# A two-layer retention / mLSTM trunk: 38 groups of mixer projections rewritten as seven half-size products, with one pool of weight tiles

## The chip, the cores and the metric

The kernel runs on one core of one Trainium2 chip. The metric is the device time of one execution in microseconds (us), as the median of several runs. PE is TensorE (PEld its weight loads), DVE is VectorE, ACT is ScalarE, POOL is GpSimd, SP is SyncE, which issues most DMAs.

## The reference

A residual stream `x` of 512 positions by 1024 channels passes two layers. Each has a token mixer (layer 0: retention, layer 1: mLSTM) and a convolutional feed-forward net (FFN). Each of the four is normalised and modulated by the condition `c`:

```
mod = silu(c) @ ada_w[i] + ada_b[i]                 # 6 x 1024 modulations of a layer
h   = rmsnorm(x, norm_tok_g[i]) * (1 + sc_t) + sh_t
x   = x + gt_t * mixer(h)                           # retention or mLSTM, 4 heads
h   = rmsnorm(x, norm_ffn_g[i]) * (1 + sc_f) + sh_f
x   = x + gt_f * (silu(a) * b) @ w_down             # a, b = causal_dwconv(h @ w_up)
```

A mixer projects `h` to queries and keys (256 columns a head each), values and gates (512 columns a head each), forms causal scores (512 by 512), weights the values with them, normalises by head, gates, and multiplies with `w_out`. The change touches only how the projections `h @ w_in` of the mixers are computed, and where the modulations stand.

## The kernel before

**Number format.** Every float32 operand is split into a high part, rounded to the type that PE multiplies in one pass (`F32R`), and a low part, the rest. A product is three matmuls: high by high, high by low, low by high (`mm3`, line 585). For weights, ACT rounds the high part (`high_part`, 467) and DVE subtracts it from the loaded tile (`low_part`, 472). `low_part_added` (477) makes the low part without DVE: ACT writes minus the high part, and a DMA issued by POOL adds the loaded tile to it.

**Two ways to project.** `proj_item` (673) makes 128 output channels for all 512 positions: 8 slices of the contraction, three matmuls each, 24 matmuls 512 wide. Before, all queries, keys and gates of the mixers go this way. `v_items` (819) makes the 512 value columns of a head with 96 matmuls 512 wide. In the FFN, `folded` (682) takes two weight tiles at a time and halves positions and contraction, and computes the four quarter products by seven products of half size and sums (the Strassen-Winograd scheme): per product 4 slices and three matmuls 256 wide, so 84 for a pair of tiles. `Fold` (518) prepares its weights: sums of halves on DVE (`ws`, `wt`), three rounded tiles on ACT, low parts mostly by `low_part_added`. The sums of `h` that it needs (`t24`, `t3`) come from `Start.sums` (982) and `turn` (1005). After some products ACT copies a partial result out of PSUM (`fs`) and DVE adds it back to another quarter.

**Order.** `heads` (1124) lists the work of a mixer's four heads: projections, scores (`S`), weighting (`A_`), normalisation (`mid_`, `end_`), output pieces (`o`). The code records calls on tiles; `Plan` (139) then orders each engine's calls by due times and its own estimates of durations and free buffers, and issues them. Each engine runs its list strictly in that order. The FFN's folded part and the start (`ret_start`, 1373) keep a written order (`plan.pin`). All calls are issued at line 367, so all rows of the profile have that line; tiles are told by name: `pp` is a PSUM bank of `proj_item`, `pv` of values, `p` of a folded pair, `pav` of weighting, `psc` of scores, `po` of outputs; `whi`/`wlo` are weight parts, `raw` a loaded tile, `ada` a modulation's weights.

**Buffers.** Weights have three pools: 6 `raw`, 8 `whi`, 8 `wlo`. Activations have 55 slots of 512 columns.

**Modulations.** 96 rows of `ada` (128 by 1025) are each loaded by SP and reduced by one DVE instruction (`gemv`, 446). 16 are done in the start; `side_work` (450) hangs the other 80 on items of the work (lines 1692 to 1706): until 24 are left (`LATER`) during retention, the rest in the mLSTM.

Of the kernel before, what the change touches and what calls it, by code (L numbers as in the profile page):

```python
# [16 lines left out]
P = 128  # L17
# [11 lines left out]
WBUFS = 8  # L29
RAWS = 6  # L30
LATER = 24
FOLD_FROM = 5
# [8 lines left out]
NSLOTS = 55  # L41
# [3 lines left out]
KINDS = {"s": NSLOTS, "whi": WBUFS, "wlo": WBUFS, "raw": RAWS, "a": 2, "ps": 8, "vm": 4, "dsh": 4}  # L45
# [325 lines left out]
def trunk(ctx: ExitStack, tc: tile.TileContext, xT, cb, pos, vec, ident, decay, zmask, ada, w_s0, w_in0, w_v0,  # L371
          w_o0, w_in1, w_v1, w_o1, w_up, w_dn, out):
# [3 lines left out]
    wpool = ctx.enter_context(tc.tile_pool(name="wpool", bufs=WBUFS))  # L376
    raws = ctx.enter_context(tc.tile_pool(name="raws", bufs=RAWS))
# [18 lines left out]
    def wide(s, dt=F32):  # L396
        if dt == F32:
            return tile_of(raws, [P, D + 1], F32, "raw", s)
        return tile_of(wpool, [P, WCOLS + WPAD], dt, s[:3], s)
# [26 lines left out]
    c_row = wide("c_row")  # L426
# [40 lines left out]
    def high_part(w, r, off=0):  # L467
        hi = wide(uid("whi"), F32R)[:, off + r.start : off + r.stop]
        A.copy(hi, w[:, r])
        return hi  # L470

    def low_part(w, hi, r, off=0):
        lo = wide(uid("wlo"), F32R)[:, off + r.start : off + r.stop]
        V.tensor_tensor(lo, w[:, r], hi.bitcast(F32), op=ALU.subtract)
        return lo

    def low_part_added(w, hi, r, off=0):

        lo = wide(uid("wlo"), F32R)[:, off + r.start : off + r.stop]
        A.mul(lo, hi.bitcast(F32), -1.0)  # L480
        G.dma_start(lo.bitcast(F32), w[:, r], accum_op=ALU.add)
        return lo

    class Chunk:
        def __init__(self, src, n, off):
            self.raw, self.r, self.off = wide(uid("raw")), slice(0, n), off
            S.dma_start(self.raw[:, self.r], src)

        def high(self):
            self.hi = high_part(self.raw, self.r, self.off)  # L490

        def low(self):
            self.lo = low_part(self.raw, self.hi, self.r, self.off)
# [4 lines left out]
    class Beside(Chunk):  # L498
# [3 lines left out]
        def __init__(self, src):  # L502
            self.raw, self.r, self.off = aside("raw"), slice(0, WCOLS), 0
            S.dma_start(self.raw[:, :WCOLS], src)

        def low(self):
            n = 3 * P
            self.lo = wide(uid("wlo"), F32R)
# [9 lines left out]
    class Fold:  # L518


        def __init__(self, src):
            self.src, self.p, self.hi = src, {}, {}

        def load(self):
            src = self.src
            self.a, self.b = wide(uid("wa")), wide(uid("wb"))
            S.dma_start(self.b[:, :WCOLS], src[1])
            S.dma_start(self.a[:, :WCOLS], src[0])

        def high(self, w, *names):  # L530
            self.hi[names] = high_part(w, slice(0, WCOLS), OFF)

        def low(self, w, low, *names):
            hi = self.hi[names]
            lo = low(w, hi, slice(0, WCOLS), OFF)
# [9 lines left out]
        def sums_13(self):  # L545
            a, b = self.a, self.b
            s = self.s13 = wide(uid("ws"))
# [3 lines left out]
        def sums_24(self):  # L551
            s = self.s24 = wide(uid("wt"))
            V.tensor_tensor(s[:, :T], self.s13[:, :T], self.a[:, :T], op=ALU.subtract)
            V.tensor_tensor(s[:, T:WCOLS], self.a[:, T:WCOLS], s[:, :T], op=ALU.subtract)
# [13 lines left out]
        def high_b(self):  # L568
            self.bp = wide(uid("whi"), F32R)[:, OFF : OFF + WCOLS]
            A.copy(self.bp[:, :T], self.b[:, T:WCOLS])  # L570

        def low_b(self):
            bp = self.bp
            V.tensor_tensor(bp[:, T:], self.b[:, T:WCOLS], bp[:, :T].bitcast(F32), op=ALU.subtract)
            self.p[4] = (bp, 0, bp, T)

    class Pair:
# [3 lines left out]
        def split(self, src, r=slice(None), eng=None):  # L581
            A.copy(self.hi[:, r], src)
            (eng or V).tensor_tensor(self.lo[:, r], src, self.hi[:, r].bitcast(F32), op=ALU.subtract)

# [48 lines left out]
    def scaled(k, r, rs, layer, which, xg=None, xr=None):  # L633

        xr = xr or slot("xr")
        if xg is None:
            V.scalar_tensor_tensor(xr[:, r], x[k][:, r], gain_col(layer, which, k), rs[:, r],
                                   op0=ALU.mult, op1=ALU.mult)
# [1177 lines left out]
```

## Time and profile before

| | |
|---|---|
| time, median of 3 runs | 1524.46 us (1522.66 to 1524.97) |
| profiled execution: its span, first to last instruction | 1521.7 us (what lies around the span isn't listed for it; the median is 2.8 us above) |
| PE busy | 1505.3 us (99%), 9037 matmuls |
| DVE busy | 1198.3 us (79%), 1832 instructions |
| ACT busy | 865.1 us (57%) |
| POOL busy | 218.8 us (14%) |
| granted PE clock | 0.998 |

The work lies in this order: start to 66 us, retention's other work to about 406, boundary (norms) to 444, FFN 0 to 754, boundary to 785, mLSTM to 1156, boundary to 1193, FFN 1 to 1500, end. Matmul durations overlap, since matmuls are pipelined: a 512-wide one is listed with 389 ns, yet 48 of them follow each other in 10.9 us. A busy share near 100% on PE therefore says that PE is never without work, and the chain of waits tells how fast it goes.

### The profile page before, as it was taken

To read this page: it belongs to the slowest core of one execution; us is meant where nothing else is said; L and a number is where in the kernel's file an instruction comes from. 1 tells how busy PE (TensorE), PEld (TensorE's weight loads), DVE (VectorE), ACT (ScalarE), POOL (GpSimd) and SP (SyncE) were. 2 spreads that over 40 slices of the span, in tenths; PEclk is the share of its full clock that TensorE was granted. 3 is DMA by queue.
4 is the path that set the end of the run, shared out by engine and by line. 5 is a ranking of instruction groups with operands and counts; after the bars stand their busy time and mean duration, and the time that the engine had idled before them with its cause. 6 is when DMAs were issued, how large, how long until landed. Compare 5 with 4: busy or idle time off the path is not lost.

```text
span 1521.7 us, 23272 instructions
## 1 busy us (share of the span) xinstructions
PE 1505.3 (99%) x9037; PEld 1340.7 (88%) x9037; DVE 1198.3 (79%) x1832; ACT 865.1 (57%) x1286; POOL 218.8 (14%) x232
## 2 busy tenths in 40 slices
PE   9999999999999999999999999999999999999997
PEld 6888888888998999999988888888889889999997
DVE  6996878777998777877867986858598967877785
ACT  4625424344566767676666662545545667776763
POOL 0021011220220111111200111010022211111102
PEclk9999999999999999999999999999999999999999
DMA  8814456555336787777425235152333357868751
GB/s 291 314 42 173 148 194 212 187 187 205 128 98 169 186 212 181 194 182 173 158 70 201 71 143 175 42 201 84 124 125 101 95 141 198 205 174 196 181 140 56
DMA packets 72370, 241.87 MB, mean 159 GB/s; under 512 B 9906, under 2 KB 12338, under 8 KB 72259
## 3 DMA queue, kind: packets, MB, share of 16 engines
q1 hardware_dynamic: 59874, 195.28, 36.3%
q0 software_dynamic: 12384, 45.09, 16.4%
q8 instruction: 71, 1.16, 0.3%
q14 instruction: 41, 0.33, 0.1%
HBM read 193.13 MB, written 2.12 MB: 128 GB/s over the span
## 4 chain that ended last, share of the span: by engine, by line
PE 95%; DVE 3%; DMA 1%; issue 1%; ACT 0%; POOL 0%; SPq 0%; DVEq 0%; POOLq 0%; ACTq 0%
PE po L367 26%; PE pp L367 25%; PE p L367 20%; PE pv L367 10%; PE pav L367 4%; PE pf L367 3%; PE pst L367 3%; PE psc L367 2%; DMA wlo<-ws 1%; PE pc L367 1%; DVE xr L367 1%; PE pms L367 1%; DVE hl L367 1%; DVE rs L367 0%; DVE wlo L367 0%
## 5 line engine op out<-in xcount | busy, mean ns | idle before, releaser
L367 DVE TENSOR_TENSOR wlo<-raw,whi 128x1024 fp32r<-128x1024 f32 (+2 forms) x229 | 246.3, 1091 | 63.4 <-ACT whi L367 63.0
L367 ACT CAST whi<-raw 128x1024 fp32r<-128x1024 f32 (+1 forms) x197 | 200.8, 1029 | 63.8 <-PE po L367 25.9
L367 PE MATMUL pp<-hl,whi 128*128 128x512 f32 x552 | 214.8, 389 | 0.0
L367 PE MATMUL pp<-hh,whi 128*128 128x512 f32 x552 | 214.8, 389 | 0.0
L367 PE MATMUL pp<-hh,wlo 128*128 128x512 f32 x552 | 214.7, 389 | 0.0
L367 DVE SCALAR_TENSOR_TENSOR x<-po,mod,x 128x512 f32<-128x512 f32 (+1 forms) x184 | 113.9, 629 | 65.9 <-PE po L367 62.5
L367 PE MATMUL po<-ggl,whi 128*128 128x512 f32 (+1 forms) x448 | 153.2, 343 | 0.0
L367 PE MATMUL po<-ggh,wlo 128*128 128x512 f32 (+1 forms) x448 | 153.0, 343 | 0.0
L367 PE MATMUL po<-ggh,whi 128*128 128x512 f32 (+1 forms) x448 | 152.1, 343 | 0.0
L367 PE MATMUL p<-hh,wlo 128*128 128x256 f32 x544 | 150.4, 276 | 0.8 <-DMA wlo<-ws 0.8
L367 PE MATMUL p<-hh,whi 128*128 128x256 f32 (+1 forms) x546 | 150.4, 276 | 0.0
L367 PE MATMUL p<-hl,whi 128*128 128x256 f32 x544 | 150.2, 276 | 0.0
L367 DVE SCALAR_TENSOR_TENSOR ada<-ada,c_ext 128x1025 f32<-128x1025 f32 x96 | 118.6, 1237 | 5.2 <-DMA ada<-ada 5.2
L367 PEld LDWEIGHTS pp<-hh,wlo 128*128 128x128 f32 x552 | 103.6, 188 | 21.6
L367 PEld LDWEIGHTS pp<-hl,whi 128*128 128x128 f32 x552 | 103.6, 188 | 21.3
L367 PEld LDWEIGHTS pp<-hh,whi 128*128 128x128 f32 x552 | 103.6, 188 | 21.2
L367 PE MATMUL po<-yh,whi 128*128 128x256 f32 (+1 forms) x354 | 115.9, 328 | 0.0
L367 PE MATMUL po<-yl,whi 128*128 128x256 f32 (+1 forms) x352 | 115.7, 329 | 0.0
L367 PE MATMUL po<-yh,wlo 128*128 128x256 f32 (+1 forms) x352 | 115.6, 329 | 0.0
L367 ACT ACTIVATE cv<-p,vecs 128x512 f32<-128x512 f32 x68 | 53.1, 780 | 88.8 <-PE p L367 55.6
L367 PEld LDWEIGHTS p<-hh,wlo 128*128 128x128 f32 x544 | 102.1, 188 | 1.2 <-DMA wlo<-ws 1.2
L367 DVE SCALAR_TENSOR_TENSOR cv<-p,vecs,cv 128x511 f32<-128x511 f32 (+1 forms) x136 | 101.0, 745 | 2.4
(262 smaller groups left out, 3891.6 us busy)
## 6 DMA issues: line engine op xcount, KB each, us to landing
ada<-ada SPq DMA_DIRECT2D x96, 512.5 KB, 4.0
raw<-w_in SPq DMA_DIRECT2D x61, 512.0 KB, 4.7
wa<-w_up SPq DMA_DIRECT2D x34, 512.0 KB, 6.0
wb<-w_up SPq DMA_DIRECT2D x34, 512.0 KB, 5.2
wlo<-wa POOLq DMA_DIRECT2D x34, 512.0 KB, 4.6
wlo<-ws POOLq DMA_DIRECT2D x34, 512.0 KB, 5.3
raw<-w_o SPq DMA_DIRECT2D x32, 512.0 KB, 5.9
raw<-w_dn SPq DMA_DIRECT2D x32, 512.0 KB, 5.7
```

The lines of the kernel that those rows point to most:

```text
L367: getattr(c.obj, c.name)(*[real(v) for v in c.a], **{key: real(v) for key, v in c.k.items()})
```

## The change

1. **Groups by seven products.** Queries and keys of retention heads 1 to 3 and of all four mLSTM heads (14 groups of two tiles), gates of heads 1 to 3 in both mixers (12 groups) and values of heads 1 to 3 in both (6 heads, two groups each): 38 groups. `fold_pairs` does pairs of tiles, `fold_values` values; `seven` runs the products in the order 1, 2, 6, 5, 7, 4, 3. Retention head 0's projections, mLSTM's first gates and its head-0 values stay as they were.
2. **Sums of `h`** become a class `Sums`, built once more for retention (after head 0's queries and keys) and for the mLSTM (its `Start` is now `folded`).
3. **One pool** of 18 weight tiles replaces 6 + 8 + 8; the activation slots grow from 55 to 62.
4. **x reloaded.** `x`'s slots are given back after the first norm, and 8 DMAs load it again before the first output pieces.
5. **Modulations.** During retention they stop at 48 left (before: 24); 16 move into FFN 0's folded units, one a unit; the other 32 (before: 24) into the mLSTM.

The core of the diff:

```diff
-WBUFS = 8
-RAWS = 6
+WTILES = 18
 LATER = 24
+MIDDLE = 24
+FREE_STEPS = (0, 3)
+VADDED = (1, 6, 7)
-NSLOTS = 55
+NSLOTS = 62
...
+        def prepare(self):
+            self.load()
+            self.high_a()
+            self.low_a()
+            a, b = self.a, self.b
+            u, v = (wide(n)[:, OFF : OFF + WCOLS] for n in ("ws", "wt"))
+            V.tensor_tensor(u[:, T:WCOLS], b[:, :T], b[:, T:WCOLS], op=ALU.add)
+            V.tensor_tensor(u[:, :T], u[:, T:WCOLS], a[:, :T], op=ALU.subtract)
+            V.tensor_tensor(v[:, :T], a[:, :T], b[:, :T], op=ALU.subtract)
+            V.tensor_tensor(v[:, T:WCOLS], a[:, T:WCOLS], u[:, :T], op=ALU.subtract)
+            self.high(u, 6, 5)
+            self.low(u, LOWS[self.added](low_part, low_part_added), 6, 5)
+            self.high(v, 7, 3)
+            self.low(v, low_part_added, 7, 3)
+            self.high_b()
+            self.low_b()
...
+    class ValueFold:
...
+            for n, i, j, op in ((5, 3, 4, ALU.add), (6, 5, 1, ALU.subtract), (7, 1, 3, ALU.subtract),
+                                (8, 2, 6, ALU.subtract)):
+                raw[n] = wide("ws")[:, OFF : OFF + WCOLS]
+                V.tensor_tensor(raw[n], raw[i], raw[j], op=op)
+            for name, r in ((1, 1), (2, 2), (6, 6), (5, 5), (7, 7), (4, 4), (3, 8)):
+                hi = high_part(raw[r], OFF)
+                self.p[name] = hi, (low_part_added if name in VADDED else low_part)(raw[r], hi, OFF)
...
+    ORDER = (1, 2, 6, 5, 7, 4, 3)
...
+                for s, f in zip(streams, fs):
+                    o = {1: s.c21, 2: s.c11, 5: s.c12, 3: s.c12}.get(n, s.c21)
+                    s.product(n, o, n in s.starts)
+                    if n in (1, 6, 7):
+                        A.copy(f[:, HB if n == 6 else HA], s.c21)
+                    if n == 7:
+                        V.tensor_tensor(s.c22, s.c12, f[:, HA], op=ALU.add)
+                    elif n == 2:
+                        V.tensor_tensor(s.c11, s.c11, f[:, HA], op=ALU.add)
+                    elif n == 3:
+                        V.tensor_tensor(s.c12, s.c12, f[:, HB], op=ALU.add)
...
     def ret_g(i):
-        for j in range(4):
-            proj_item(w_in0[i * 8 + 4 + j], h0, ret_gate(i))
+        fold_pairs(pair_srcs(w_in0, i * 8 + 4), sums0.terms, [ret_gate(i)] * 2)
+
+    def ret_v(i, between=nothing):
+        fold_values(w_v0[i - 1], sums0.terms, R[i]["v"], center_split, between)
...
             product(i, 1, c2[:, HA], True)
+            for _ in range(len(side) - LATER > 0 and i < len(folds) - 1):
+                pin, plan.pin = plan.pin, None
+                side_work(*side.pop(0), gate)
+                plan.pin = pin
```

`fold_pairs` alternates `added` by pair, so every other pair makes the low part of `u` on DVE.

What this does to the engines' lists is seen at three places. The first is DVE where retention's head 0 gets its scores: PE's scores need the four `qkl` (low parts of rotated queries and keys). Before, these rows of DVE lead there (`rp` are the products of the rotation, from the banks `pp`):

```order
L367 TENSOR_TENSOR rp_837<-pp_714,cos_817 128x512
L367 TENSOR_TENSOR rp_843<-pp_747,sin_815 128x512
L367 TENSOR_TENSOR rp_850<-pp_603,sin_815 128x512
L367 TENSOR_TENSOR rp_858<-pp_661,cos_817 128x512
L367 TENSOR_TENSOR rp_863<-pp_714,sin_815 128x512
L367 TENSOR_TENSOR rp_870<-pp_747,cos_817 128x512
L367 TENSOR_TENSOR qkl_875<-rp_831,qkh_855 128x512
L367 TENSOR_TENSOR qkl_883<-rp_837,qkh_868 128x512
```

After the change the same place reads:

```order
L370 TENSOR_TENSOR whi_705<-wb_522,whi_705 128x512
L370 TENSOR_TENSOR p_188_817<-p_187_836,fs_840 128x256
L370 TENSOR_TENSOR rp_944<-pp_612,sin_871 128x512
L370 TENSOR_TENSOR rp_952<-pp_669,cos_868 128x512
L370 TENSOR_TENSOR rp_960<-pp_720,sin_871 128x512
L370 TENSOR_TENSOR rp_973<-pp_771,cos_868 128x512
L370 TENSOR_TENSOR ws_935<-ws_935,wa_608 128x512
L370 SCALAR_TENSOR_TENSOR vl_989<-vt_597,vm_598,vh_742 128x512
L370 SCALAR_TENSOR_TENSOR vl_1001<-vt_631,vm_632,vh_757 128x512
L370 SCALAR_TENSOR_TENSOR vl_1011<-vt_638,vm_639,vh_766 128x512
L370 SCALAR_TENSOR_TENSOR vl_1022<-vt_648,vm_649,vh_776 128x512
L370 TENSOR_TENSOR qkl_1033<-rp_909,qkh_937 128x512
```

A pair's sums (`ws`), the rest part of a `wb`, and an addition to a PSUM bank now stand among the rotations, and the value parts (`vl`) follow; the four `qkl` come a few rows later. Up to the fourth `qkl`, DVE's list has 31 instructions more than before: 25 for the new set of sums of `h` with `turn`, 9 for sums and rests of the first two groups' weights, 2 additions, and 5 fewer others.

The second place is PE inside the first changed group (`p_188` and `p_187` are its two banks): product 7 (operand `t3`) is followed at once by product 4 (operand `t24`).

```order
L370 MATMUL p_188_817<-t3h_884,whi_682 128x256
L370 MATMUL p_188_817<-t3l_898,whi_682 128x256
L370 MATMUL p_188_817<-t3h_884,wlo_692 128x256
L370 MATMUL p_188_817<-t24h_709,whi_705 128x256
L370 MATMUL p_188_817<-t24l_774,whi_705 128x256
L370 MATMUL p_188_817<-t24h_709,whi_705 128x256
```

Between these two products ACT copies the bank and DVE adds to it, and product 4 waits for both. In 21 of the 26 pairs the planner put 10 or more 256-wide matmuls (or as much of other work) between them; in five there is less than 0.5 us of it.

The third place is DVE in the mLSTM, where the weights of head 1's gates are made. Before:

```order
L367 TENSOR_TENSOR wlo_9093<-raw_8956,whi_9022 128x1024
L367 SCALAR_TENSOR_TENSOR yl_9101<-z_8738,vecs,yh_9090 128x512
L367 TENSOR_TENSOR wlo_9107<-raw_9025,whi_9054 128x1024
L367 SCALAR_TENSOR_TENSOR ada_9040,mod_90<-ada_9040,c_ext 128x1025
L367 TENSOR_TENSOR wlo_9124<-raw_9066,whi_9105 128x1024
L367 TENSOR_SCALAR gain_92<-mod_90,vecs 128x1
L367 TENSOR_TENSOR wlo_9153<-raw_9118,whi_9146 128x1024
```

After:

```order
L370 TENSOR_TENSOR wlo_10431<-ws_10319,whi_10349 128x1024
L370 TENSOR_TENSOR ws_10446<-wb_10218 128x512
L370 TENSOR_TENSOR ws_10446<-ws_10446,wa_10211 128x512
L370 TENSOR_TENSOR p_1775_10422<-p_1775_10422,fs_10418 128x256
L370 TENSOR_TENSOR den_10222<-den_10222,db_10048 128x512
L370 TENSOR_TENSOR wt_10481<-wa_10211,wb_10218 128x512
L370 TENSOR_TENSOR wt_10481<-wa_10211,ws_10446 128x512
L370 TENSOR_TENSOR whi_10342<-wb_10097,whi_10342 128x512
L370 SCALAR_TENSOR_TENSOR ada_10083,mod_87<-ada_10083,c_ext 128x1025
```

Where DVE made one low part for each tile, it now makes four half-width sums, a rest part and three additions to PSUM for each pair, and a low part for every other pair.

More of the change, by code (lines that the diff above doesn't have):

```diff
@@ L423, in trunk @@
         ones[name] = o
[L426 removed]
+    c_row = wide("c_row")[:, :D]
     S.dma_start(c_row[:1, :D], cb)
@@ L1245, in items @@
             downs = [p for gi in range(len(GROUPS) - 1) for p in self.down(gi)]
-            steps, run = folded(folds, self.h, self.start.terms, pairs, downs)
+            steps, run = folded(folds, self.h, self.start.sums.terms, pairs, downs)
             def early(n):
@@ L1703, in trunk @@
         late = n > bars[0]
-        for _ in range((n % 2) if late else (2 if n > 20 and n % 5 == 0 else 1)):
-            if len(side) > (0 if late else LATER):
-                side_work(*side.pop(0), gate)
+        turn += 1
+        if len(side) > (0 if late else LATER + MIDDLE) and (not late or turn % 3):
+            side_work(*side.pop(0), gate)
     assert not side
```

441 lines of the change are left out of this document (269 added, 172 removed).

## Prediction

> **What bounds the kernel now.** I read the totals of the page first, then busy time by stretch, then the chain that ended last, and then the price of single operations.
>
> ```profile
> span 1521.7 us, 23272 instructions
> PE 1505.3 (99%) x9037; PEld 1340.7 (88%) x9037; DVE 1198.3 (79%) x1832; ACT 865.1 (57%) x1286; POOL 218.8 (14%) x232
> PEclk9999999999999999999999999999999999999999
> q0 software_dynamic: 12384, 45.09, 16.4%
> ```
>
> PE is without work for 1521.7 - 1505.3 = 16.4 us in all, at full clock. DVE comes next. The next rows are stretches of the span; the columns are length, then busy us (and instructions) of PE, PEld, DVE, ACT, POOL, clock, DMA share and GB/s.
>
> ```profile
> 40.00:66.00 26.00, 26.00 (x117) 21.52 (x116) 25.86 (x40) 13.56 (x16) 0.62 (x1) 1.00 0.94 326
> 66.00:86.00 20.00, 20.00 (x90) 16.57 (x89) 17.70 (x31) 9.65 (x18) 1.25 (x4) 1.00 0.46 169
> 400.00:500.00 100.00, 99.02 (x678) 91.38 (x677) 90.45 (x153) 64.30 (x107) 18.84 (x22) 1.00 0.47 131
> 66.15:406.18 340.03, 340.03 (x1672) 289.83 (x1672) 274.76 (x399) 143.54 (x226) 55.59 (x51) 1.00 0.49 170
> 443.80:754.00 310.20, 309.70 (x2190) 287.88 (x2190) 245.52 (x389) 216.02 (x303) 40.64 (x47) 1.00 0.70 179
> 785.17:1155.69 370.52, 370.52 (x1806) 314.96 (x1805) 277.09 (x391) 197.96 (x285) 41.45 (x38) 1.00 0.37 128
> ```
>
> The fourth and sixth are the two mixers: PE never waits there, and DVE is busy 81% and 75%. The fifth is FFN 0, the model for the change: the same scheme, PE full, DMA share 0.70. From the chain (start, length, what):
>
> ```profile
> 98.79 3.86 PE psc L367 x24
> 102.65 10.91 PE pp L367 x48
> 121.26 21.78 PE pv L367 x96
> 504.73 8.17 PE p L367 x72
> 1233.35 9.63 DMA wlo<-ws
> ```
>
> 48 matmuls of 512 columns take 10.91 us (227 ns each), 72 of 256 columns 8.17 us (113.5 ns): half the width, half the time.
>
> **The change part by part: PE.** A group goes from 48 x 0.227 = 10.89 us to 84 x 0.1135 = 9.53 us, a saving of 1.36 us. 18 groups in retention give 24.5 us, 20 in the mLSTM 27.2, together 51.7. PE has 340.0 - 24.5 = 315.5 us left in retention's stretch and 370.5 - 27.2 = 343.3 in the mLSTM's.
>
> The Trainium skill speaks against a gain in full proportion: its page "TensorE: Matmul & The Clock Gate", section "Back-to-back issue gap", gives N/2.4 + 2.5 ns for one matmul of N columns, a fixed part that 84 narrow ones pay more often than 48 wide ones. By it a group would go from 10.36 to 9.17 us, 1.19 us saved, 45 us in all. The two rows above show no fixed part, so the trace disagrees and the sum keeps 51.7.
>
> **DVE.** Prices: rows by form give durations (second number after the bar, in ns). Neighbours overlap a little; the timeline shows the real steps.
>
> ```profile
> L367 DVE TENSOR_TENSOR wlo<-raw,whi 128x1024 fp32r<-128x1024 f32 x149 | 190.1, 1280 | 50.0 <-ACT whi L367 49.6
> L367 DVE TENSOR_TENSOR ws<-wb 128x512 f32<-128x512 f32 x34 | 23.3, 684 | 6.4 <-DMA wlo<-wt 6.2 <-DMA wlo<-ws 0.2
> L367 DVE TENSOR_TENSOR p<-p,fs 128x256 f32<-128x256 f32 x68 | 29.1, 428 | 26.8 <-PE p L367 26.6 <-ACT whi L367 0.2
> L367 DVE SCALAR_TENSOR_TENSOR t<-xr,mod,xr 128x256 f32<-128x256 f32 x8 | 3.3, 470 | 0.0
> L367 DVE TENSOR_TENSOR t24l<-t,t24h 128x512 fp32r<-128x512 f32 x8 | 5.4, 675 | 0.0
> L367 DVE TENSOR_TENSOR t3l<-xr,t3h 128x256 fp32r<-128x256 f32 x8 | 3.3, 408 | 0.0
> ```
> ```profile
> 41.10 1.22 DVE L367 TENSOR_TENSOR wlo<-raw,whi 128x1024 fp32r<-128x1024 f32 x1
> 42.23 1.22 DVE L367 SCALAR_TENSOR_TENSOR ada<-ada,c_ext 128x1025 f32<-128x1025 f32 x1
> 43.38 0.74 DVE L367 SCALAR_TENSOR_TENSOR hl<-xr,mod,hh 128x512 fp32r<-128x512 f32 x1
> ...
> 509.28 0.68 DVE L367 TENSOR_TENSOR ws<-wb 128x512 f32<-128x512 f32 x1
> 509.88 0.69 DVE L367 TENSOR_TENSOR ws<-wa,wb 128x512 f32<-128x512 f32 x1
> ```
>
> So a 1024-wide low part costs 1.13 us, a modulation 1.15, a 512-wide sum 0.60; additions to PSUM I take at 0.43. A pair adds five 512-wide operations (3.0), three additions (1.28) and a low part every second time (0.57) and drops two low parts (2.26): +2.59 us. The values of a head add four 1024-wide sums (4.52) and six additions (2.57), with four low parts before and after: +7.1. The sums of `h`, once a mixer: four times 3 x 0.47 + 0.68 + 0.41, and `turn`'s four 0.42: 11 us.
>
> - Retention: 274.8 + 12 x 2.59 + 3 x 7.1 + 11 - 21 modulations x 1.15 = 314. With some overlap at DVE's 41 idle pieces there, 311 us, against 315.5 of PE.
> - mLSTM: 277.1 + 14 x 2.59 + 3 x 7.1 + 11 + 8 x 1.15 = 355, say 350, against 343.3 of PE.
>
> This is the heart of the prediction: **DVE's work becomes as long as PE's**, above it in the mLSTM. How full can DVE run? From 40 to 66 us it is busy 25.86 of 26.00 (0.995) with PE never waiting, in an order written by hand; where the planner orders, the fullest stretch is 400 to 500 with 0.905. Additions that wait for PE and ACT block DVE's list, so I take 0.96, nearer to the first because what is left to do is always ready somewhere in the list. Retention 311/0.96 = 324 us, mLSTM 350/0.96 = 365 us. Ends: at 0.995 313 (so PE decides: 315.5) and 352; at 0.905 344 and 387.
>
> **Waits of PE that are new.** At the entry of retention DVE has, before head 0's scores, about 11 + 9 x 0.60 + 0.9 - 5 = 12 us more. Before, its last `qkl` came with no slack:
>
> ```profile
> 98.25 0.68 DVE L367 TENSOR_TENSOR rp<-pp,cos 128x512 f32<-128x512 f32 x1
> 98.86 0.67 DVE L367 TENSOR_TENSOR qkl<-rp,qkh 128x512 fp32r<-128x512 f32 x1
> ```
>
> It ended at 99.5, while the scores began at 98.79. DVE's idle 2.3 us between 66 and 86 and 24 matmuls that now lie ahead (2.7) take 5 of the 12: **7 us of wait**. Inside a pair, product 4 waits for ACT's copy and DVE's addition after product 7. In FFN 0 the copy starts 0.20 after PE and takes 0.37:
>
> ```profile
> 512.94 0.37 ACT L367 COPY fs<-p 128x256 f32<-128x256 f32 x1 [0.20 <-PE p L367]
> ```
>
> With the addition (0.43) that is 1.0 us. Where the order puts 10 or more matmuls (1.13 us) between, it is covered unless DVE's or ACT's list has something in front; in five pairs (two in retention) it isn't, 0.6 to 1.0 us each: 2 us a mixer. Retention's PE comes to 315.5 + 7 + 2 = 324.5, its DVE to 324: gain 340.0 - 324.5 = **15.5 us**. The mLSTM's PE comes to 345, its DVE to 365: gain **6 us**.
>
> **What costs nothing, and its cover.** ACT adds to a pair two casts and two or three more 1.05-us passes, three copies of 0.37 and half a cast, less two casts: 5.4 us; to a head's values 8.6. Retention 143.5 + 97 = 240, mLSTM 198 + 108 = 306: below PE. 77 more accumulating DMAs: 86 of them took 16.4% of 1521.7 us, 2.9 us each, so 44 in the mLSTM raise its DMA share from 0.37 to about 0.72, the value of FFN 0, where PE is full. Their landing there:
>
> ```profile
> L367 POOL DMA_DIRECT2D wlo<-wa x34: 859/859/1030, 449.8 to 1456.6; - x34
> DMA to landing us min/median/max: 4.5/5.1/10.0
> ```
>
> POOL gets 33 to 44 issues of 0.86 us a mixer, at most 38 us on 56. FFN 0 takes 13 more modulations (15 us) on 245.5 of 310.2, 0.84 full, with 24 matmuls as cover at the joints: 0 to 5 us, I take 0. The common pool of 18 tiles may start loads later or earlier: the wait of 9.63 us for `wlo` in the chain at an FFN's entry leaves PE with 0.5 us idle now, so from nothing to 10 us at each, I take 0; a gain is bounded by the same 0.5. Reloading x adds eight DMAs on SP, needed only by the first output pieces: 0, or 5 us if late. SP's 24 modulation loads that move leave a quieter queue in retention.
>
> **Sum.** 1521.7 - 15.5 - 6 = 1500.2; with the 2.8 us by which the median stands above the span, **1503 us**. Its own range, with DVE 0.93 to 0.98 full, is 1490 to 1521.
>
> **The rivals.**
>
> 1. *PE stays the bound.* My additions are taken at their duration, and DVE reached 0.995 once. Then only the entry and the joints are lost: 51.7 - 11 = 41, 1484 us, at best 1473. For: PE is full in FFN 0 with the same scheme. Against: DVE is 0.79 full there, not 1.0.
> 2. *DVE becomes a bound that costs more than PE saves (slower).* Its 311 + 350 = 661 us replace 340.0 + 370.5 = 710.5 of PE; the point is a DVE 0.93 full. At 0.905, 344 + 387 - 710.5 = +20: 1545 us. For: 0.905 is the fullest that the planner's order shows. Two things could push it there: lists blocked behind an addition that waits for ACT, and POOL. DVE's low parts beside POOL's rotations take longer than the same in the mLSTM:
>
> ```profile
> L367 DVE TENSOR_TENSOR qkl<-rp,qkh 128x512 fp32r<-128x512 f32 x16 | 15.1, 960 | 4.1 <-ACT qkh L367 4.0
> L367 DVE TENSOR_TENSOR mqkl<-mc,mqkh 128x512 fp32r<-128x512 f32 x16 | 11.4, 714 | 1.4 <-ACT mqkh L367 1.4
> ```
>
> The Trainium skill ("SBUF — State Buffer", "Who interferes with whom") says that an instruction of VectorE with two SBUF inputs contends with one of GpSimd that reads SBUF; nearly all of the added DVE work has two. These two rows agree; if the added work met as much, it would end in this rival.
> 3. *Low parts come late.* Where heads begin, nothing else of PE is at hand, and the chain load, cast, sum, cast, accumulate is longer than before. With half of the 10.0 us worst landing uncovered at the seven group starts of heads, 20 us beyond hiding, 1523 us.
>
> **How the numbers follow.** Forecast 0.49, rival 1 0.25, rival 2 0.18, rival 3 0.08. Within 0.2% (3 us, about what can be told from no change) lie the edges of rivals 2 and 3: 0.06. Faster: 0.49 + 0.25 + 0.03 = 0.77. Slower: 0.17. The range reaches to most of rival 1 and half of rival 2: 1478 to 1536.
>
> **What would show it.** Right: in the mLSTM's stretch DVE is above 0.93 busy and PE below it, with waits for DVE in the chain (additions `p<-p,fs`, low parts, sums); retention loses some 7 us before its first scores; the matmuls keep 113.5 ns; FFN 0 and 1 keep their lengths. Wrong: PE full in both mixers (rival 1), DVE full and the mLSTM longer than 370 us (rival 2), or DMA `wlo` in the chain inside the mixers (rival 3).

## The result and the profile after

The change made the kernel **slower: 1637.07 us (1631.19 to 1638.06) against 1523.56 us (1522.46 to 1524.97), ratio 1.0737 with a 95% interval of 1.0718 to 1.0756.** The profiled execution has a span of 1635.9 us, 114.2 above the one before. The prediction of 1503 us missed by 134 us, and its range by 101.

The page of the changed kernel: totals, the clock by slices, and the queue of the accumulating DMAs (packets, MB, share of 16 DMA engines).

```profile
span 1635.9 us, 26855 instructions
PE 1517.3 (93%) x10405; PEld 1403.2 (86%) x10405; DVE 1328.5 (81%) x2111; ACT 1039.8 (64%) x1573; POOL 300.0 (18%) x323
PEclk9999989899999999999999999999999999999999
q0 software_dynamic: 24336, 88.62, 29.0%
```

PE was without work for 118.6 us, where it had 16.4 before, and the clock row has dips that the row of before doesn't have. Stretches of the changed kernel follow, in the columns of the prediction (length, then busy us of PE, PEld, DVE, ACT and POOL, granted clock, DMA share, GB/s). They run from retention's first `pp`, and then from the first `pf` of FFN 0, of the mLSTM and of FFN 1 (`pf` is the bank of the first projections after each norm). I write them in the order of the view: retention, mLSTM, FFN 0, FFN 1.

```profile
66.40:448.30 381.90, 348.96 (x2436) 326.90 (x2435) 325.68 (x495) 238.89 (x381) 97.51 (x95) 0.96 0.66 182
811.00:1240.00 429.00, 398.59 (x2839) 373.32 (x2838) 383.18 (x606) 308.53 (x477) 88.28 (x97) 0.97 0.67 178
448.30:811.00 362.70, 350.03 (x2444) 323.92 (x2443) 290.83 (x475) 233.12 (x339) 51.98 (x58) 0.99 0.70 182
1240.00:1635.90 395.90, 356.67 (x2449) 329.15 (x2447) 274.85 (x445) 229.66 (x339) 53.26 (x63) 0.97 0.57 141
```

Cut at the same matmuls, the kernel before has 353.8, 408.9, 340.9 and 352.0 us. Its FFN 1:

```profile
1169.70:1521.70 352.00, 341.42 (x2449) 318.14 (x2447) 272.78 (x435) 228.02 (x333) 53.14 (x63) 0.99 0.60 155
```

So the loss is everywhere: 28 us in retention, 20 in the mLSTM, 22 in FFN 0, and **44 in FFN 1, where the change has no operation of its own**. That last number speaks against the groups as the only cause.

One place in FFN 1 shows how such a stage loses. DVE of the changed kernel (start, length, what, and in brackets the idle time before it and what ended it):

```profile
1409.49 0.75 DVE L370 SCALAR_TENSOR_TENSOR x<-po,mod,x 128x512 f32<-128x512 f32 x1 [0.89 <-PE po L370]
1415.57 1.22 DVE L370 TENSOR_TENSOR wlo<-wt,whi 128x1024 fp32r<-128x1024 f32 x1 [5.33 <-DMA wlo<-wa]
1416.72 0.42 DVE L370 TENSOR_TENSOR p<-p,fq 128x256 f32<-128x256 f32 x1
```

PE, ACT and POOL at the same place:

```profile
1417.20 0.39 PE L370 MATMUL p<-t24h,whi 128*128 128x256 f32 x1 [3.62 <-DVE p L370]
```
```profile
1408.64 1.05 ACT L370 CAST whi<-wt 128x1024 fp32r<-128x1024 f32 x1 [0.57 <-DVE wt L370]
1410.86 0.38 ACT L370 COPY fq<-p 128x256 f32<-128x256 f32 x1 [1.17 <-PE p L370]
```
```profile
1405.38 0.86 POOL L370 DMA_DIRECT2D wlo<-wa  x1 [8.22 <-PE p L370]
```

PE waits 3.62 us for an addition to PSUM (`p<-p,fq`). That addition takes 0.42 us, and ACT had made its `fq` by 1411.24; it is late only because it stands behind a low part in DVE's list. The low part has its inputs, `wt` and (since 1409.69) `whi`; what it waits for, 5.33 us, is the DMA of **another** product, the one that adds `wa` to `wa`'s own low part and was issued at 1405.38. Its result needs a tile, and by the program's addresses the tile that this `wlo` gets is the one that `wa` had: until that DMA has read `wa`, DVE may not write. Before, this couldn't happen: `wa` lay in the pool of loaded tiles, a low part in another. There DVE stands idle for `fq` alone, and adds as soon as it is made:

```profile
1402.26 0.43 DVE L367 TENSOR_TENSOR p<-p,fq 128x256 f32<-128x256 f32 x1 [1.02 <-ACT fq L367]
```

The view of waits says how often (us in total, times, longest). ACT of the changed kernel:

```profile
ACT wlo L370 <- DMA wlo<-wa: 47.9, 16, 4.9
ACT whi L370 <- DMA wlo<-wt: 31.9, 7, 9.3
ACT wlo L370 <- DMA wlo<-ws: 20.6, 6, 7.3
ACT whi L370 <- DMA wlo<-ws: 14.1, 12, 3.5
```

DVE of the changed kernel:

```profile
DVE p L370 <- ACT fq L370: 53.6, 16, 5.7
DVE wlo L370 <- DMA wlo<-wa: 27.1, 9, 5.3
```

All waits of ACT and DVE for a DMA `wlo` come to 158 us, against 6.4 us in the kernel before. And some of PE's stalls are paid in part a second time: after them the profile has 16 stretches at half clock. Three successive stretches of PE at FFN 1's entry, where it waited 1.68 us for DVE at 1252 (length, PE busy, clock, DMA share, GB/s):

```profile
1250.90:1254.30 3.40, 1.63 (x12) 1.00 0.12 47
1254.40:1257.70 3.30, 3.30 (x18) 0.50 0.00 0
1257.80:1261.20 3.40, 3.40 (x32) 1.00 0.00 0
```

For 3.3 us after the wait PE ran at half clock, and 18 matmuls lie in that stretch; the 3.4 us behind it have 32.

To separate these things I counted PE's time by matmuls: their columns at the full pace (227 ns for 512, in proportion for fewer), then what half clock added to those that started under it, then the rest, which is waits and slower matmuls. FFN 1 goes to its last matmul here; some 10 us of the end, without PE, are in its length and not in this table.

| us: full pace + half clock + rest | retention | FFN 0 | mLSTM | FFN 1 |
|---|---|---|---|---|
| before | 352.0 + 0 + 1.7 | 336.8 + 0 + 4.1 | 405.1 + 0 + 4.0 | 337.4 + 0 + 5.0 |
| after | 327.6 + 8.5 + 45.9 | 337.0 + 4.6 + 21.2 | 377.6 + 7.0 + 44.3 | 337.6 + 9.4 + 39.4 |

The matmuls' count fell as planned (24.4 and 27.5 us). The rest rose by 136 us, half clock by 30.

### The profile page after: what moved, and what is told of

The parts are those of the page before. It is cut to its first block, busy times and chain, and to the rows that moved or that the text cites. A ratio compares the mean times of both kernels' runs of the same rounds, so it can differ in the third digit from the quotient of the medians.

```text
span 1635.9 us, 26855 instructions
## 1 busy us (share of the span) xinstructions
PE 1517.3 (93%) x10405; PEld 1403.2 (86%) x10405; DVE 1328.5 (81%) x2111; ACT 1039.8 (64%) x1573; POOL 300.0 (18%) x323
## 5 line engine op out<-in xcount | busy, mean ns | idle before, releaser
L370 PE MATMUL p<-hh,whi 128*128 128x256 f32 (+1 forms) x962 | 273.3, 285 | 0.6 <-DVE vl L370 0.6
L370 PE MATMUL p<-hl,whi 128*128 128x256 f32 x960 | 272.2, 284 | 0.0
L370 PE MATMUL p<-hh,wlo 128*128 128x256 f32 x960 | 270.6, 283 | 1.2 <-DMA wlo<-wa 1.2
L370 ACT ACTIVATE wlo<-whi 128x1024 fp32r<-128x1024 f32 x169 | 179.2, 1062 | 79.4 <-DMA wlo<-wa 47.9
L370 PE MATMUL p<-t24h,whi 128*128 128x256 f32 x720 | 171.1, 294 | 60.5 <-DVE p L370 41.7
L370 PEld LDWEIGHTS p<-t24h,whi 128*128 128x128 f32 x720 | 127.9, 196 | 75.1 <-DVE p L370 54.1
L370 PEld LDWEIGHTS p<-hh,whi 128*128 128x128 f32 x962 | 187.8, 195 | 1.5 <-PE psc L370 0.7
L370 PEld LDWEIGHTS p<-hl,whi 128*128 128x128 f32 x960 | 187.0, 195 | 0.3
L370 DVE TENSOR_TENSOR wlo<-raw,whi 128x1024 fp32r<-128x1024 f32 (+2 forms) x153 | 154.4, 1032 | 15.7 <-ACT whi L370 8.7
L370 ACT CAST whi<-raw 128x1024 fp32r<-128x1024 f32 (+1 forms) x121 | 122.2, 1021 | 37.6 <-DVE wlo L370 11.6
L370 PE MATMUL p<-t24l,whi 128*128 128x256 f32 x480 | 137.6, 287 | 0.0
```

What stands on the lines that cost most here:

```text
L370: getattr(c.obj, c.name)(*[real(v) for v in c.a], **{key: real(v) for key, v in c.k.items()})
```

## The experiments

**Theory A**: the common pool couples ACT's and DVE's lists to transfers that they have nothing to do with. Rivals: **B**, 18 tiles are too few, however divided; **C**, the groups fill DVE's and ACT's lists; **R3** (the prediction's third rival), the groups' low parts land late; **D**, the modulations in FFN 0.

Stage lengths of all runs, from their traces, and the ratio to the kernel before (95% interval):

| run | retention | FFN 0 | mLSTM | FFN 1 | median us | ratio |
|---|---|---|---|---|---|---|
| before | 353.8 | 340.9 | 408.9 | 352.0 | 1523.56 | 1 |
| after | 381.9 | 362.7 | 429.0 | 395.9 | 1637.07 | 1.0737 (1.0718 to 1.0756) |
| p1 before, one pool | 353.8 | 391.5 | 409.3 | 399.4 | 1621.71 | 1.0638 (1.0617 to 1.0660) |
| p2 before, 6 + 6 + 6 | 353.8 | 347.8 | 409.6 | 360.2 | 1538.90 | 1.0097 (1.0082 to 1.0112) |
| p3 after, no groups | 353.9 | 369.8 | 409.7 | 399.7 | 1593.71 | 1.0467 (1.0435 to 1.0499) |
| p4 after, 6 + 6 + 6 | 370.1 | 365.3 | 424.6 | 367.8 | 1597.52 | 1.0483 (1.0454 to 1.0511) |
| q1 after, planner's tiles | 363.2 | 346.8 | 408.3 | 359.6 | 1548.69 | 1.0169 (1.0152 to 1.0186) |
| q2 p1, planner's tiles | 353.8 | 349.6 | 409.6 | 357.7 | 1539.31 | 1.0101 (1.0086 to 1.0116) |
| q3 p4, few rows added | 355.5 | 363.6 | 404.4 | 368.0 | 1562.55 | 1.0261 (1.0239 to 1.0284) |
| q4 p4, modulations back | 372.7 | 366.6 | 416.7 | 367.4 | 1587.82 | 1.0424 (1.0400 to 1.0448) |
| r1 q1, small modulations | 356.5 | 346.0 | 413.8 | 358.0 | 1542.89 | 1.0124 (1.0109 to 1.0139) |
| r2 q1, few rows added | 356.7 | 347.5 | 402.8 | 360.4 | 1537.09 | 1.0087 (1.0070 to 1.0103) |
| r3 q1, both | 350.8 | 346.5 | 400.3 | 359.3 | 1525.79 | 1.0014 (1.0004 to 1.0023) |
| r4 q1, 19 tiles | 360.7 | 350.8 | 411.1 | 360.0 | 1551.34 | 1.0174 (1.0159 to 1.0190) |
| t1 q1, later landings | 358.5 | 347.1 | 407.4 | 358.7 | 1539.60 | 1.0096 (1.0077 to 1.0114) |
| t2 pairs only | 354.0 | 352.8 | 402.1 | 361.0 | 1539.54 | 1.0103 (1.0088 to 1.0118) |
| t3 mLSTM only, 20 tiles | 360.2 | 351.7 | 416.9 | 363.5 | 1558.64 | 1.0230 (1.0215 to 1.0245) |
| t4 before, own pick | 353.9 | 340.2 | 409.4 | 351.8 | 1523.39 | 1.0000 (0.9991 to 1.0010) |
| u1 before, pad 16 | 359.1 | 348.2 | 416.7 | 359.9 | 1552.99 | 1.0195 (1.0178 to 1.0212) |
| u2 mLSTM only, pad 64 | 353.8 | 353.0 | 402.5 | 357.2 | 1533.82 | 1.0072 (1.0057 to 1.0087) |

### The pool by itself, and without its sharing

p1 gives the kernel before the common pool and the 62 slots of the change:

```diff
-WBUFS = 8
-RAWS = 6
+WTILES = 18
-NSLOTS = 55
+NSLOTS = 62
...
-        if dt == F32:
-            return tile_of(raws, [P, D + 1], F32, "raw", s)
-        return tile_of(wpool, [P, WCOLS + WPAD], dt, s[:3], s)
+        return tile_of(wpool, [P, WCOLS + WPAD], dt, "w", s)
```

> The kernel before, in which only the buffers change: one common pool of 18 weight tiles and 62 activation slots, no group, no moved modulation. Theory A (the common pool couples engines to transfers: ACT or DVE writes into a buffer whose last reader is an accumulating DMA, its list stands until that DMA lands, and the PSUM copies and additions behind it come late): FFN 1 loses most of the 41 us that it lost in the change, FFN 0 some 20, the mixers, which have no accumulating DMA here, 0 to 5: 1570 to 1590 us. Theory B (18 tiles are too few, however they are divided): about the same here, 1560 to 1600. Theory C (the groups themselves fill DVE's and ACT's lists, and the pool costs nothing): 1524 within 5 us.

p2 keeps three pools and cuts them to as many tiles:

```diff
-WBUFS = 8
+WBUFS = 6
-NSLOTS = 55
+NSLOTS = 62
```

> The kernel before with its three pools kept apart, but cut to 6 loaded, 6 high and 6 low tiles: 18 in all, as many as the common pool, and 62 slots. Theory A: no engine writes into a buffer that an accumulating DMA still reads, since such buffers go to loads or sums only: 1520 to 1540 us, far below the common pool. Theory B: as slow as the common pool, 1560 to 1600. Theory C: 1524 within 5.

**98.6 us against 15.8, with 18 tiles in both.** The common pool alone, without a single group, costs most of what the change costs; A had the places right (both FFNs, 51 and 47 us; the mixers, which have no accumulating DMA there, 0) and little more than half of the size. For this kernel B fails, and C fails as the only cause. (In p1, p2 and p4 the planner, with other room, also orders DVE's and ACT's lists a little differently; q1 and q2, below, don't have that difference.) The waits of ACT and DVE for a DMA `wlo` are 130 us in p1, 12 in p2.

p3 undoes the groups in the changed kernel and keeps the rest; queries, keys and the values go back in the same way:

```diff
-        fold_pairs(pair_srcs(w_in0, i * 8 + 4), sums0.terms, [ret_gate(i)] * 2)
+        for j in range(4):
+            proj_item(w_in0[i * 8 + 4 + j], h0, ret_gate(i))
```

> The changed kernel with all 38 groups undone (queries, keys, values and gates by whole tiles as before); the pool of 18, the 62 slots, the reloaded x and the moved modulations stay. Theory A: as the kernel before with one pool, plus what the 13 modulations cost in FFN 0 (up to 15): 1570 to 1600 us. Theory C: 1520 to 1540, so that the groups cost the other 100.

p4 keeps the groups and divides the 18 tiles:

```diff
-WTILES = 18
+RAWS, HIGHS, LOWERS = 6, 6, 6
...
+        if dt == F32:
+            return tile_of(raws, [P, WCOLS + OFF], dt, "raw", uid(s))
+        pool, tag = (highs, "whi") if s == "whi" else (lowers, "wlo")
+        return tile_of(pool, [P, WCOLS + WPAD], dt, tag, uid(s))
```

> The changed kernel with all its groups, its 18 tiles divided into 6 loaded, 6 high and 6 low ones. Theory A: the FFNs go back to within 10 us of their lengths before and the 7 us waits for ACT in the mixers go: 1500 to 1550 us. Theory B: 1600 to 1660. Theory C: FFNs back, but the mixers as long as in the change (50 us over what PE needs): 1560 to 1590.

p3 agrees with A, and its mixers are as long as before: the x that is loaded again, the slots and the modulations cost them nothing. (Why its FFN 0 is 22 us shorter than p1's isn't shown; the two order their lists differently.) p4 agrees with none: FFN 1 gets 28 us back, FFN 0 nothing, the mixers 12 and 4. Something else holds it up as well: its matmuls are slower (below, at the pad), and DVE waits 42 us for the accumulating DMAs before it may write the sums `ws` and `wt`, against 12 in p2. With the groups, six tiles for loads and sums are few, so a part of B stays.

### Which tile is taken

The planner reckons that a new buffer takes the tile that by its times comes free first. The pool itself hands tiles out in nearly the order in which the written program gives them back (851 of 1126 times the one given back longest ago), and there a tile counts as given back where its last instruction stands, for an accumulating DMA where it is issued. With one kind of buffer in a pool both come to about the same; with loads, sums, high and low parts in one pool they don't. q1 makes the planner's pick the real one, with every engine's list the same:

```diff
-        room = {key: [0.0] * n for key, n in KINDS.items()}
+        room = {key: [(0.0, i) for i in range(n)] for key, n in KINDS.items()}
...
-                        room[b.key].pop(0)
+                        b.at = room[b.key].pop(0)[1]
...
-            self.real = pool.tile(shape, dt, tag=tag, name=name)
+            self.real = pool.tile(shape, dt, tag=f"{tag}{self.at}" if self.key == "w" else tag, name=name)
```

(each tag then has one tile). q2 does the same to p1.

> The changed kernel, each engine's list word for word the same; only which of the 18 tiles a new buffer takes is now the planner's own pick, the one that by its times comes free first, instead of the one that was given back longest ago in the written order (which counts a buffer as free once its accumulating DMA is issued, not landed). Theory A1 (the wrong tile is taken, one whose DMA is still reading): both FFNs come back to within 10 us of their 341 and 352 before, the mixers lose 10 to 20 of their waits: 1540 to 1575 us. Theory A2 (any common pool of 18 couples the lists like this, whichever tile is taken): 1620 to 1640.

> The kernel before with one common pool of 18 tiles and the planner's own pick of the tile. Theory A1: most of the 98 us of the common pool go: 1525 to 1550 us. Theory A2: 1600 to 1622.

**88 us of the change's loss and 82 of p1's are gone, with no instruction moved: A1, the wrong tile is taken.** Which tile is taken also moves addresses, but that isn't the gain: PE's waits fall by some 66 us, half clock by 24, and slower matmuls by 1. ACT of q1 waits for these DMAs in four rows, 16 us in all where it was 125:

```profile
ACT whi L370 <- DMA wlo<-wt: 6.4, 2, 5.4
ACT whi L370 <- DMA wlo<-ws: 4.7, 3, 2.4
ACT whi L370 <- DMA wlo<-wa: 4.6, 3, 2.0
ACT wlo L370 <- DMA wlo<-ws: 0.3, 1, 0.3
```

ACT and DVE still write into tiles that such a DMA has read, 140 times against 145; the DMA has now mostly landed. t4 gives the kernel before the same pick inside its three pools, with the later landings of t1:

> The kernel before, its three pools of 6, 8 and 8 kept, with the planner's own pick within each pool and the later landings; no other change. If the same wrong pick costs it anything (its two FFNs have 4 and 5 us of stalls): 1515 to 1521 us. If not: 1522 to 1526.

No difference: where kinds are kept apart, nothing was lost by it.

### What is left: 25 us

In q1 the FFNs are 6 and 8 us over before, the mLSTM 1 under, retention 9 over, where the forecast had it 15 under. Stretches of q1, retention and mLSTM:

```profile
66.10:429.30 363.20, 342.97 (x2436) 321.33 (x2435) 321.92 (x494) 239.13 (x381) 97.87 (x95) 0.99 0.69 193
776.10:1184.40 408.30, 393.21 (x2839) 368.96 (x2839) 382.43 (x606) 307.64 (x477) 88.14 (x97) 0.99 0.70 189
```

DVE is 0.89 and 0.94 busy. Four runs take load away and keep the lists. q3 (on p4) and r2 (on q1) let the groups' accumulating DMAs carry 8 of 128 rows; r1 cuts the modulations to 64 of 1025 columns, and r3 does both (`n` is 8 in the first cut, 64 in the second):

```diff
-        G.dma_start(lo.bitcast(F32), raw, accum_op=ALU.add)
+        c = G.dma_start(lo[:n].bitcast(F32), raw[:n], accum_op=ALU.add)
+        c.dma = P * raw.width * 4e-6 * 5.4 + 0.05
...
-        return V.scalar_tensor_tensor(raw, raw, 1.0, c_ext[:], op0=ALU.mult, op1=ALU.mult,
+        return V.scalar_tensor_tensor(raw[:, :n], raw[:, :n], 1.0, c_ext[:, :n], op0=ALU.mult, op1=ALU.mult,
```

> The changed kernel with three pools of 6, in which the accumulating DMAs of the 38 groups add 8 of the 128 rows (so low parts of the other rows are wrong: left out); same lists, same planner's costs, only these transfers are a sixteenth. Theory R3 (the mixers wait for low parts that land late): retention and mLSTM each 25 to 40 us shorter than the 370 and 425 with whole transfers: 1525 to 1550 us. Theory C (DVE's and ACT's lists, and the joints in a group, hold PE up): within 10 us of the 1597 with whole transfers.

> The changed kernel with the planner's own pick of the tile (1549 us), in which the 80 modulations after the start take 64 of their 1025 columns (so the modulations are wrong: left out); lists and planner's costs the same. That takes some 1 us of DVE for each: 24 in retention, 16 in FFN 0, 40 in the mLSTM and its boundaries. Theory C1 (DVE, 0.94 busy in the mLSTM and 0.89 in retention, is what the mixers wait for): mLSTM 15 to 25 us shorter, retention 8 to 15: 1508 to 1525 us. Theory C2 (each addition and copy is late by its own latency and by what stands ahead on ACT; DVE's load matters little): 1540 to 1549.

> The changed kernel with the planner's own pick of the tile, its groups' accumulating DMAs cut to 8 of 128 rows (other rows' low parts wrong: left out). Theory R3 (the mixers wait for low parts): retention and mLSTM each 12 to 20 us shorter, 1510 to 1525. If what is left of the mixers' waits has other causes: 3 to 6 each, 1537 to 1545.

> Both cuts of the two runs before it together. If DVE's load and the transfers stand in for each other (either one alone leaves the other as the wait): more than the sum of the two, 1490 to 1505 us. If they are separate waits: the sum of the two. If neither is what the mixers wait for: 1535 or more, and the joints alone are left.

(The modulations' counts by stage in the text of r1 are off: 32, 16 and 32. DVE has 30 us less to do in retention and 31 in the mLSTM.)

q3 gained 35 us, 15 of it in retention and 20 in the mLSTM, about half of what R3 expected: there the low parts do come late. With the right tiles they matter less: r2 gains 12 us (6.5 and 5.5 in the mixers). r1 gains 6 where C1 had 24 to 41; its mLSTM even got 6 longer, which no run explains. Together they gain 23, some 5 more than their sum; q1's own runs spread over 4.6 us, so this is a hint and no more that the loads of DVE and of the transfers stand in for each other in part. Neither is what the mixers mainly wait for. **Even without both, r3 is no faster than the kernel before**, though its PE has 52 us less to do. Its mixers keep 23 and 21 us of rest. The first wait in retention, DVE of r3 and then PE:

```profile
95.92 0.68 DVE L370 TENSOR_TENSOR rp<-pp,sin 128x512 f32<-128x512 f32 x1
96.52 0.68 DVE L370 TENSOR_TENSOR ws<-wb 128x512 f32<-128x512 f32 x1
97.11 0.68 DVE L370 TENSOR_TENSOR whi<-wb,whi 128x512 fp32r<-128x512 f32 x1
97.72 0.42 DVE L370 TENSOR_TENSOR p<-p,fs 128x256 f32<-128x256 f32 x1
```
```profile
98.19 0.38 PE L370 MATMUL p<-t24h,whi 128*128 128x256 f32 x1 [2.24 <-DVE p L370]
```

The addition between products 7 and 4 stands behind a product of the rotation, a sum for another group, and the rest part that product 4 itself reads. PE's waits inside q1's retention are mostly of this kind:

```profile
PE p L370 <- ACT fs L370: 6.2, 4, 2.4
PE p L370 <- DVE p L370: 4.8, 5, 2.2
PE p L370 <- DMA wlo<-wt: 2.6, 1, 2.6
PE pav L370 <- ACT sh L370: 1.9, 2, 1.0
PE pv L370 <- DVE pv L370: 1.9, 2, 1.1
```

The other part of the rest is slower matmuls. In FFN 0 six products of a folded pair, 72 matmuls, took 8.17 us before, 113.5 ns each. Two products of 12 in the mLSTM of q1, from its chain:

```profile
988.29 2.83 PE p L370 x24
1103.97 2.83 PE p L370 x24
```

That is 118 ns each; the mean of such matmuls in q1's mixers is 116. Matmuls that start up to a quarter of a microsecond late make 9.4 and 9.9 us of the rest in q1's mixers, 1.7 and 2.1 before: 15.5 us that the count of columns doesn't show. About 10 of them are matmuls less than 0.1 us late, as here; the others are short waits.

q4 puts the modulations of p4 back:

```diff
-MIDDLE = 24
+MIDDLE = 0
```

> The changed kernel with three pools of 6 and the modulations where they were before (24 left after retention, none in FFN 0). Theory D (the modulations inside FFN 0 hold DVE's additions up): FFN 0 falls from 365 to 345 to 350 us, retention grows by 5 to 15 since DVE has 28 us more there: 1585 to 1600. If the modulations cost nothing in FFN 0: 365 stays, and the whole is 1600 to 1615.

FFN 0 doesn't change; the mLSTM, which has 8 modulations fewer, is 8 us shorter, retention 3 longer. D fails; r1 says the same (FFN 0 0.8 us shorter).

t1 tells the planner that transfers land 2 us later:

```diff
-                c.end = dma_free + 0.9
+                c.end = dma_free + 2.9
...
-        return c.lat if not c.dma else 2.4 + c.dma
+        return c.lat if not c.dma else 4.4 + c.dma
```

> The changed kernel with the planner's own pick of the tile, and a planner that reckons every transfer to land 2 us later than it did (the traces show 5.7 to 7.6 us from issue to landing where its rule gives 3.4 for a load and 5.0 for an accumulating one). Theory E (what is left of the mixers' waits comes from lists ordered by landings that are too early): retention and mLSTM 5 to 12 us shorter each, 1526 to 1540 us. If the order is not at fault, only tiles are held longer: 1546 to 1560.

9 us, of which 5 in retention and 1 in the mLSTM: E holds in sign, and only retention comes near its size. In t1 the units of the FFN have come back to their time, 8.17 us for six products and 15.04 from unit to unit, as before:

```profile
558.75 8.17 PE p L370 x72
573.79 8.17 PE p L370 x72
588.83 8.17 PE p L370 x72
```

Of what is left of the FFNs' loss there, 6 and 7 us, some 4 have arisen within 70 us of the first `pf` (from there to the same product: 88.8 us against 84.4 in FFN 1), and it stays at that up to some 300 us (299.1 against 295.5 in FFN 0).

### More tiles, fewer groups, and a pad

r4 has 19 tiles, t2 only the 26 pairs with 19 tiles, t3 only the mLSTM's groups with 20 and 60 slots; t2 and t3 also have t1's landings and the modulations back. To fit, each cuts the tiles' pad:

```diff
-WTILES = 18
+WTILES = 19
...
-WPAD = 64
+WPAD = 16
```

(In t2 the values by whole tiles read an `h` whose first four slices already hold the turned halves, so its values are not the reference's.)

> The changed kernel with the planner's own pick and 19 tiles instead of 18 (each tile's pad cut from 64 to 16 columns to make room). Theory B2 (what is left of the FFNs' loss, 6 and 8 us, and some of the mixers' waits, come from too few tiles): 1535 to 1542 us. If the number of tiles is not what is waited for: within 3 of 1549.

> Later landings and own pick, 19 tiles (pad 16), modulations back where they were, and values by whole tiles again: only the 26 pairs of queries, keys and gates stay as groups (35 us of PE by the matmuls' count). Theory C1 (DVE's and the transfers' load is the price, and values pay most of it: 7.1 us of DVE for 2.7 of PE a head): 1518 to 1532 us. If the pairs pay as badly: 1535 to 1548.

> Later landings and own pick, 20 tiles (pad 16), 60 slots, modulations back, groups in the mLSTM alone; retention by whole tiles. Retention as before (354 us), the FFNs 3 to 8 us each over before, the mLSTM between 398 and 408 against 409 before: 1520 to 1532 us. Under 1520 only if the mLSTM's groups keep half of their 27 us.

r4 looks as if a tile more were worth nothing, t2 as if pairs paid as badly as values, and t3 is 27 us or more over what I expected, with a retention 6 us longer than before although it has no group. u1 is the control, the kernel before with the pad cut:

> The kernel before with the pad of its weight tiles cut from 64 to 16 columns, nothing else: lists the same. It is the control for the runs with 19 and 20 tiles. If the pad (the address at which a tile begins) sets the pace of matmuls, 512-wide ones go from 227 to 231 ns and 256-wide ones from 113 to 117 or 118, as in those runs: 25 to 35 us more, 1548 to 1560 us. If it does not: 1524 within 3.

The pad alone costs 29.7 us, with the same lists. From the chain of u1, the 96 value matmuls that took 21.78 us before, and 72 of a folded pair that took 8.17:

```profile
123.47 22.20 PE pv L367 x96
496.55 8.60 PE p L367 x72
```

231 and 119 ns a matmul in place of 227 and 113.5. So r4, t2 and t3 measure the pad too. In r4 the slower matmuls took 20 us more than in q1, while PE's waits fell by 16: a 19th tile seems to help, and its pad eats that. p4's pools lie at other addresses, too, with the pad of 64, and its matmuls are as slow as u1's, 96 of 512 columns and 72 of 256:

```profile
68.18 22.32 PE pp L370 x96
1331.89 8.60 PE p L370 x72
```

That is some 9 us in each of its FFNs, and part of why p4 disappointed; no run moves its pools alone. p2 keeps its pace within 2 us in each FFN. In its FFN 0, which is 7 us longer than before, PE has some 33 delays of 0.1 to 0.4 us, 5 us in all, most of it at the first matmuls with `t24`, which wait for an addition.

u2 repeats t3 with the pad of 64 and 18 tiles:

> The groups in the mLSTM alone with the pad of 64 as in the change, 18 tiles, 62 slots, later landings, own pick, modulations back: the run of 20 tiles without its pad. If the pad was what made that run slow (1559): retention 354, the FFNs 346 and 358, the mLSTM 402 to 408, 1526 to 1536 us. If the groups or the moved waits made it slow: 1545 or more. Below 1523 only if the mLSTM's groups gain over 12 us, which nothing so far shows.

The mLSTM takes 402.5 us, 6.4 less than before: **there the groups do gain, a quarter of their 27 us.** FFN 0 loses 12 of it and FFN 1 five. No version here beats the kernel before; of those that compute the whole with groups, u2 (1.0072) and t1 (1.0096) come nearest.

## Why the prediction was wrong

**The step that failed** is in "What costs nothing": *"The common pool of 18 tiles may start loads later or earlier: ... from nothing to 10 us at each, I take 0."* I asked only when loads start, so only at an FFN's entry. The pool also decides what else a tile's next writer must wait for, in every unit of both FFNs and in the mixers. q1 against the change puts 88 us on it, of the 134 by which I missed: 19 in retention, 16 in FFN 0, 21 in the mLSTM, 36 in FFN 1, half clock after the stalls included (a clock of 0.973 against q1's 0.992); by stages of the two profiled executions it is 92. What would have found it is to ask of each buffer what ACT or DVE write next into a tile that an accumulating DMA still reads, and what stands behind that in their lists. A row of the prediction had such a wait: 6.2 us of DVE's `ws` for DMA `wlo<-wt`.

The rest of the miss, by q1: retention 363.2 us against 353.8 - 15.5 = 338.3, **25 us**; the FFNs **13 us**; the mLSTM 408.3 against 402.9, **5 us**. With the 88 that is 131 or 132 of 134.

- *PE saves 51.7 us*: by columns 51.9. As time 36 to 42, since narrow matmuls in the mixers took 116 ns in the mean and up to 118, not the 113.5 of FFN 0 that I carried over. The Trainium skill ("TensorE: Matmul & The Clock Gate", "Back-to-back issue gap") spoke for 45 us, because narrow matmuls pay a fixed part more often. The mixers went the way that it says, but not by its rule: the formula gives 109 ns for 256 columns, under both figures, and FFN 0 shows no fixed part. What makes them slower stays open.
- *DVE's work*: right. I added 36 us in retention and 73 in the mLSTM; the stretches went from 288.1 to 325.7 and from 308.8 to 383.2, 37.6 and 74.4. (That nearly all of it has two SBUF inputs is not so: the additions, over a quarter of a pair's, have one of theirs in PSUM.)
- *DVE 0.96 full*: wrong as a way to get the time. DVE was 0.85 and 0.89 full; with the right tiles 0.89 and 0.94. And its fullness was not the wait: r1 took about 1 us from each of 80 modulations and gained 6.
- *A wait of 7 us before the first scores*: half of it. In q1 PE waits 2.2 us at the first group's joint and 1.0 before the scores. *Joints, 2 us a mixer*: too low. Waits for `fs` and `p` are 11 us in q1's retention and 6 in the mLSTM, since DVE's and ACT's lists have other work in front where I had counted 10 matmuls as cover.
- *mLSTM gains 6 us*: 0.6 in q1. The 6.4 of u2 meet the number by chance: mine came from DVE's fullness, while in u2 waits and slower matmuls of PE take some 21 of the 27 us.
- *Modulations in FFN 0, the x that is loaded again*: nothing, as said (p3, q4, r1). ACT and POOL were tested by no run alone; PE's waits for ACT's `fs`, 6.2 and 4.7 us in q1's mixers, say that ACT's part was not nothing.
- *Rival 1* (PE stays the bound) fails: PE is without work for 118.6 us.
- *Rival 2*, 1545 us, lies near q1's 1549 by chance: its mechanism is not what r1 shows. *Rival 3's* sign did appear, DMA `wlo` in the chain, but mostly because of the tile. Its own price was 12 us (r2).
- *Sums that are off*: the change adds 83 accumulating DMAs (169 against 86), not 77; ACT's 5.4 us a pair holds with three casts, not the two that are named; and with DVE 0.93 to 0.98 full the terms give 1496 to 1525 us, not 1490 to 1521. None of these decides the miss.

Open: why narrow matmuls are slower in the mixers of q1, whose pad is 64 (the addresses or the traffic; no run separates them), and the mixers' last waits at the joints, which no run removed.

## What to carry to other kernels

A pool is part of the order: whoever shares one among kinds of buffers lets each writer wait for the last reader of any kind, and on an engine with a strict list everything behind it waits too. Before merging pools, list for each kind who reads it last, and keep those whose last reader is a slow DMA away from tiles that ACT or DVE write, or hand tiles out by when that DMA lands: for the kernel before, one pool with the right pick (q2, 1.0101) cost no more than three (p2, 1.0097). And a stage without a changed operation that gets longer is the best witness: compare those first.

## What the runs showed of the hardware

- **Less than 3.4 us without work can halve PE's clock.** The half-clock stretches of the changed kernel lie on one grid of 3.41 us: 11 last one step, two last two, three last three. All 13 steps at full clock in which PE was idle for 1.9 us or more are followed by one at half clock, none with less than 1.65 us is, and of the five between, three. So one wait of 1.68 us was enough at 1252, while 2.22 us at 1451.5, cut in two by the grid, were not. The Trainium skill ("TensorE: Matmul & The Clock Gate", "What's actually happening") says that PE is throttled after an idle window of about 3.4 us and that the window runs freely. The length and the grid agree; here about half a window without work was enough.
- **The pad of the weight tiles, and with it their addresses, changes the pace of matmuls**: 16 columns in place of 64 cost 2% of the kernel (1.0195, 1.0178 to 1.0212) with the same instructions; 512 columns go from 227 to 231 ns and 256 from 113.5 to between 118 and 119. Which addresses are good, the runs don't show.
- An accumulating DMA of 512 KB (`wa`, `ws` or `wt`) landed 5.8 to 7.1 us after its issue in the median of the changed kernel (4.6 to 7.2 before), and 7.0 to 7.6 in q1.
